# Sixteen subtractions of a two-layer hybrid block move from GpSimd to VectorE, with new instruction orders in five of its seven regions

## The chip, the cores and the metric

The kernel runs on one core of a Trainium2 chip. The metric is the device time of one execution in microseconds (us). TensorE is called PE, VectorE DVE, ScalarE ACT and GpSimd POOL in the views of the profile; SP is the sync engine, which issues most DMAs.

## The reference, cut to what matters

Two layers work on a latent sequence of 512 tokens and a context of 256, both 1024 wide, all in float32. Layer 0 mixes with a gated long convolution and a grouped-query attention; layer 1 with an mLSTM (a recurrence with a matrix state per head, here by chunks, forwards and backwards). Only the latent tokens of layer 1 are returned.

```python
for layer in range(2):
    need_ctx = layer < 1
    h_lat = rms_norm(x_lat, g_pre[layer]) * (1 + sc_l) + sh_l      # sc, sh, ga: silu(c) @ w_mod + b_mod
    h_ctx = rms_norm(x_ctx, g_pre[layer]) * (1 + sc_c) + sh_c
    if layer == 0:
        y_lat, y_ctx = even_mixer(h_lat, h_ctx, ...)               # convolution | attention, then @ e_w_out
    else:
        y_lat, _ = odd_mixer(h_lat, h_ctx, ...)
    x_lat = x_lat + ga_l * rms_norm(y_lat, g_post[layer])
    if need_ctx:
        x_ctx = x_ctx + ga_c * rms_norm(y_ctx, g_post[layer])
return x_lat

# the end of odd_mixer: 8 heads of 256 make the 2048 columns that o_w_out turns into 1024
h = (h_f + h_b) * sigmoid(o)
h = rms_norm(h per head, head_norm)
y = (h * silu(z)) @ w_out
```

## The kernel before, in words

*Number format.* Each float32 matmul is three matmuls on rounded parts: a tensor is split into a high part (`wh`, `hTh`, `yfh`; a cast on ACT) and a low part (`wl`, `hTl`, `yfl`; DVE subtracts the high part from the source), and `mm3` issues high x high, low x high and high x low into one PSUM tile. Weights come by DMA on SP into `wr` (three buffers, half a slot's columns each), ACT casts them to `wh`, DVE makes `wl`; there are two slots of `wh` and `wl`, each filled in two halves of 128x1024. A slot can be refilled when PE's last matmul on it has ended.

*Regions and orders.* The whole program is written down as calls first (`record`), cut into seven regions: `start`, `hy` (the convolution of layer 0), `att` (its attention), `out0` (its output product, the norms after it, and the norm and transposes of layer 1), `l1a` (the dense part, with the first products of layer 1), `l1b` (its scan), `out1` (its output product and the end). `play` then issues each region's calls in the order of a table, `ORDERS[region]`, and every engine keeps that order. So the tables fix which instruction follows which on each engine, and an engine stands when the next one in its row is not ready. A second table, `SLOTS`, says which of a pool's buffers each tile takes. All instructions carry the line L998 of `play`, so the views are read by the names of tiles. The digits behind a name in an order (`pm_8141`) tell one tile from another.

*Layer boundary (`out0`).* For each of six token tiles the norm gives `xt`, `sst`, `rs` and `xn` (two halves); eight transposes on PE turn `xn` into two PSUM tiles `pm` (four each); ACT and DVE each scale two of the four blocks into `hf`, and a split makes `hTh` and `hTl`, on which all of layer 1's products work. The first of these products are the 288 columns for gates and values (`wh1_1348`, `wl1_1349`, loaded as `wr_8192`, `wr_8193`, `wr_8194`).

*Output of layer 1.* It is computed with seven products instead of eight (p1, q7, q6, q3, q5, p2, q4) of blocks of the activations and of sums of weight blocks. The activations of the sums are the "forms". At the end of `l1b`, `raws` (`vh`, `vl`, `cvo`) hold the finished heads; they are split, and a difference of two halves of their columns is taken in place. In `out1`, `forms(h)` loads a pair of heads as `yraa` and `yrab`, and takes three differences: two in place on `yraa`, one into `yf`. The results are split into `yfh`/`yfl`, `ybh`/`ybl` and parts of `hTh`/`hTl`. These differences are the subtractions of the change; their instructions are 2 of 128x768, 2 of 128x256 and 12 of 128x512. In the last head groups of `l1b`, `hst` and `hrs` (on POOL) give the head norm's factor, `hh<-hh,hrs,zs` applies it, and PE transposes `hh`.

Of the kernel before, what the change touches and what calls it, by code (L numbers as in the profile page):

```python
# [151 lines left out]
class Ctx:  # L152
# [679 lines left out]
    ],  # L832
    "yraw@9": [
        0, 0, 0, 1, 1, 0, 1, 0,
    ],
    "ess@9": [
        0, 0, 0, 0, 0, 0,
# [2056 lines left out]
```

## Time and the profile before

| what | value |
|---|---|
| median of 3 runs | 1501.41 us (1500.29 to 1501.62) |
| profiled execution | 1502.13 us, its span 1500.4 us |
| mean granted clock of TensorE | 0.990 of full |
| PE, DVE, ACT, POOL busy | 1454.9, 1073.5, 779.8, 121.1 us |
| the 16 subtractions on POOL | 26.6 us |

The span goes from the first to the last instruction; 1.7 us of the execution lie around it. "Busy" is the time in which an engine had an instruction at work; durations overlap a little where an engine starts an instruction before the one ahead of it has ended. The granted clock is what the chip gave TensorE, 1.00 being full speed.

### The profile page before, as it was taken

The page shows a single profiled execution, that of the slowest core. Times are in us where ns is not written, and L with a number is a line of the kernel's source. Part 1 is how long each engine was busy: PE and PEld are TensorE (multiplying, and loading weights), DVE is VectorE, ACT ScalarE, POOL GpSimd, SP SyncE. Part 2 cuts the span into 40 slices and gives each one's busy share as a digit, 9 for nine tenths or more (in the row PEclk, how much of TensorE's full clock was granted, in tenths as well). Part 3 has the DMA queues.
Part 4 walks back from the last instruction along what each step waited for, and adds up shares of the span by engine and source line. Part 5 has one row for each costly group of instructions (what it writes and reads, how often), then busy time and mean ns, then how long its engine had stood idle before and what let it go on. Part 6 is the DMA issues. An engine that isn't in the chain of part 4 may idle for free. (4 is left out here: it accounts for less than half of the span.)

```text
span 1500.4 us, 25608 instructions
## 1 busy us (share of the span) xinstructions
PE 1454.9 (97%) x10122; PEld 1328.6 (89%) x10122; DVE 1073.5 (72%) x1955; ACT 779.8 (52%) x1587; POOL 121.1 (8%) x157
## 2 busy tenths in 40 slices
PE   7999999999999999999999889999999999999987
PEld 5889999889998999899997779999999999998765
DVE  6687777887866666768334789566777777877787
ACT  6634343434435444446332557654766666765553
POOL 1100000001000000010000100000102010011130
PEclk9999999999999999999999999999999999999999
DMA  9755565557231121242552334675866454574665
GB/s 378 214 136 146 148 163 128 146 139 187 70 99 48 49 96 54 81 138 92 187 208 67 116 119 155 225 248 198 238 183 135 112 167 122 169 196 155 240 204 202
DMA packets 63688, 230.95 MB, mean 154 GB/s; under 512 B 7707, under 2 KB 9243, under 8 KB 60784
## 3 DMA queue, kind: packets, MB, share of 16 engines
q1 hardware_dynamic: 55000, 198.63, 38.7%
q0 software_dynamic: 7696, 29.50, 10.8%
q8 instruction: 80, 1.31, 0.4%
q10 hardware_dynamic: 872, 1.18, 0.3%
q14 instruction: 40, 0.33, 0.1%
HBM read 207.23 MB, written 68.19 MB: 184 GB/s over the span
## 5 line engine op out<-in xcount | busy, mean ns | idle before, releaser
L998 PE MATMUL pj<-wl,hTh 128*128 128x256 f32 (+2 forms) x1104 | 316.5, 292 | 1.9 <-DVE wl L998 1.9
L998 PE MATMUL pj<-wh,hTh 128*128 128x256 f32 (+2 forms) x1104 | 315.6, 293 | 0.9 <-ACT qjunk L998 0.5
L998 PE MATMUL pj<-wh,hTl 128*128 128x256 f32 (+2 forms) x1104 | 314.7, 292 | 0.0
L998 PE MATMUL pj<-hTh,wh 128*128 128x512 f32 (+1 forms) x832 | 286.6, 346 | 0.2 <-DVE vl L998 0.2
L998 PE MATMUL pj<-hTl,wh 128*128 128x512 f32 (+1 forms) x832 | 285.6, 344 | 0.6 <-DVE hTl L998 0.6
L998 PE MATMUL pj<-hTh,wl 128*128 128x512 f32 (+1 forms) x832 | 285.4, 345 | 0.0
L998 DVE TENSOR_TENSOR wl<-wr,wh 128x1024 fp32r<-128x1024 f32 (+1 forms) x154 | 188.7, 1231 | 50.7 <-ACT wh L998 50.5
L998 PEld LDWEIGHTS pj<-wh,hTh 128*128 128x128 f32 x1104 | 207.0, 189 | 7.9 <-issue 2.1
L998 PEld LDWEIGHTS pj<-wl,hTh 128*128 128x128 f32 x1104 | 208.1, 190 | 6.6 <-DVE wl L998 2.6
L998 PEld LDWEIGHTS pj<-wh,hTl 128*128 128x128 f32 x1104 | 206.7, 189 | 3.9 <-issue 0.5
L998 ACT CAST wh<-wr 128x1024 fp32r<-128x1024 f32 (+1 forms) x154 | 159.0, 1044 | 71.8 <-PE pj L998 39.0
L998 PEld LDWEIGHTS pj<-hTh,wh 128*128 128x128 f32 x832 | 156.6, 189 | 18.7 <-DVE vl L998 0.8
L998 PEld LDWEIGHTS pj<-hTl,wh 128*128 128x128 f32 x832 | 156.7, 188 | 17.8 <-DVE hTl L998 0.9
L998 PEld LDWEIGHTS pj<-hTh,wl 128*128 128x128 f32 x832 | 156.3, 188 | 17.5 <-DVE wl L998 0.2
L998 ACT CAST PTh<-pj 128x384 fp32r<-128x384 f32 (+1 forms) x80 | 35.6, 459 | 49.3 <-PE pj L998 45.5
L998 DVE TENSOR_TENSOR PTl<-pj,PTh 128x384 fp32r<-128x384 f32 (+1 forms) x80 | 41.3, 525 | 22.5 <-ACT PTh L998 22.2
L998 DVE TENSOR_TENSOR wl<-ch,wh 128x1024 fp32r<-128x1024 f32 x28 | 34.0, 1219 | 26.2 <-ACT wh L998 26.2
L998 POOL DMA_DIRECT2D o_sums<-in_o_w_in x28 | 22.8, 814 | 334.5 <-DMA o_sums<-in_o_w_in 167.4
L998 DVE TENSOR_REDUCE mx<-s 128x1 f32<-128x768 f32 (+1 forms) x48 | 37.0, 774 | 14.7 <-PE s L998 14.6
L998 ACT ACTIVATE qjunk<-pj 128x128 f32<-128x128 f32 x60 | 16.7, 278 | 55.3 <-PE pj L998 23.4
L998 PE MATMUL s<-dfa,qTh 128*128 128x256 f32 (+1 forms) x160 | 45.0, 343 | 0.0
L998 PE MATMUL pm<-Rh,dfa 128*128 128x256 f32 (+1 forms) x192 | 45.0, 305 | 0.0
(397 smaller groups left out, 3313.6 us busy)
## 6 DMA issues: line engine op xcount, KB each, us to landing
wr<-in_e_w_in SPq DMA_DIRECT2D x52, 512.0 KB, 5.1
wr<-in_o_w_in SPq DMA_DIRECT2D x50, 512.0 KB, 5.6
o_sums<-in_o_w_in POOLq DMA_DIRECT2D x28, 512.0 KB, 6.6
ch<-o_sums SPq DMA_DIRECT2D x21, 512.0 KB, 5.7
wh<-in_w_mod SPq DMA_DIRECT2D x10, 1024.0 KB, 5.9
wl<-in_w_mod SPq DMA_DIRECT2D x9, 1024.0 KB, 8.1
wr<-in_e_w_out SPq DMA_DIRECT2D x16, 512.0 KB, 4.4
w_sums<-in_o_w_out POOLq DMA_DIRECT2D x16, 512.0 KB, 8.0
```

The lines of the kernel that those rows point to most:

```text
L998: x = fn(*a, **k)
```

## The change

The sixteen subtractions are issued on DVE instead of POOL. `ORDERS` of five regions (`att`, `out0`, `l1a`, `l1b`, `out1`) are other tables with the same calls, and `SLOTS` has other buffers for some pools (`wr`, `pj`, `pm`, `xt`, `xn`, `yraw`, `C` and others). `start` and `hy` are as they were. The number of instructions of each kind is the same but for the engine of the sixteen.

```diff
     for raw in raws:
         n = raw.shape[1]
         split(*[x[:, k:k + n, NL:NT] for x in hT_], raw[:, :, :256])
-        G.tensor_tensor(raw[:, :, 256:], raw[:, :, 256:], raw[:, :, :256], ALU.subtract)
+        V.tensor_tensor(raw[:, :, 256:], raw[:, :, 256:], raw[:, :, :256], ALU.subtract)
         k += n
...
-        G.tensor_tensor(ra[:, :, hi], ra[:, :, hi], rb[:, :, hi], ALU.subtract)
-        G.tensor_tensor(ra[:, :, lo], ra[:, :, lo], ra[:, :, hi], ALU.subtract)
+        V.tensor_tensor(ra[:, :, hi], ra[:, :, hi], rb[:, :, hi], ALU.subtract)
+        V.tensor_tensor(ra[:, :, lo], ra[:, :, lo], ra[:, :, hi], ALU.subtract)
         split(*[x[:, kk] for x in f6], ra[:, :, lo])
 
         def second():
             x = T(op, "yf3", (P, 2, 256), bufs=4)
-            G.tensor_tensor(x, rb[:, :, lo], ra[:, :, lo], ALU.subtract)
+            V.tensor_tensor(x, rb[:, :, lo], ra[:, :, lo], ALU.subtract)
```

Of the tables, `out1` has 426 entries of which 25 stand at their old place, moved by 10 places on average; `l1b` has 3871 of which 46 stand, moved by 38; `out0` 1028, 53 and 31; `att` 3139, 118 and 26; `l1a` 1701, 199 and 11. What that does is shown at three places.

DVE at the end of `l1b`, from the split of the head group that is normed last but one; `hst_11964` leads to `hrs_11965`, which the four `hh` need, and `wl_2364` is a weight half. Before:

```order
L998 TENSOR_SCALAR hst_11964<-hss_11959 128x4
L998 TENSOR_TENSOR vl_11835<-pj_11943,vh_11834 128x256
L998 TENSOR_TENSOR hTl<-vl_12057,hTh 128x3x256
L998 SCALAR_TENSOR_TENSOR hh_11945<-hh_11945,hrs_11965,zs_11839 128x256 x3
L998 SCALAR_TENSOR_TENSOR E_11966<-pm_11958,E_11966 128x512
L998 SCALAR_TENSOR_TENSOR hh_11945<-hh_11945,hrs_11965,zs_11839 128x256
L998 TENSOR_TENSOR El_11968<-E_11966,Eh_11967 128x512
L998 TENSOR_TENSOR vl_11835<-pj_11944,vh_11834 128x256
```

After:

```order
L998 TENSOR_TENSOR vl_11835<-pj_11943,vh_11834 128x256
L998 TENSOR_TENSOR vl_11835<-pj_11944,vh_11834 128x256
L998 SCALAR_TENSOR_TENSOR E_11966<-pm_11958,E_11966 128x512
L998 TENSOR_TENSOR wl_2364_11953<-wr_11954,wh_2363_11952 128x1024
L998 SCALAR_TENSOR_TENSOR hh_11945<-hh_11945,hrs_11965,zs_11839 128x256 x2
L998 TENSOR_TENSOR vl_12057<-vl_12057 128x3x256
L998 SCALAR_TENSOR_TENSOR hh_11945<-hh_11945,hrs_11965,zs_11839 128x256
L998 TENSOR_TENSOR El_11968<-E_11966,Eh_11967 128x512
L998 TENSOR_TENSOR wl_2364_11953<-wr_11955,wh_2363_11952 128x1024
L998 SCALAR_TENSOR_TENSOR C_11981<-C_11977,apb_9239,pj_11980 128x258
L998 SCALAR_TENSOR_TENSOR hh_11945<-hh_11945,hrs_11965,zs_11839 128x256
```

The subtraction of `vl_12057` stands between the `hh` on DVE; on POOL it stood ahead of two more subtractions. The split `hTl<-vl_12057`, which stood ahead of the `hh`, is further back, and a weight half stands ahead of them instead.

DVE at the start of `out1`: `wl_2496` is the second weight slot of q7, `wl_2519` that of q6, which follows it on PE; `gg` is the factor of the last norm. Before:

```order
L998 TENSOR_TENSOR wl_2496_12085<-wr_12086,wh_2495_12084 128x1024
L998 TENSOR_TENSOR wl_2496_12085<-wr_12087,wh_2495_12084 128x1024
L998 TENSOR_TENSOR gg_1586_11172<-pm_12054,gg_1586_11172 128x512
L998 TENSOR_TENSOR ybl_16007<-yrab_16011,ybh_16006 128x512
L998 TENSOR_TENSOR hTl<-yrab_16011,hTh 128x2x256
L998 TENSOR_TENSOR yfl_16005<-yraa_16010,yfh_16004 128x512
L998 TENSOR_TENSOR hTl<-yraa_16010,hTh 128x2x256
L998 TENSOR_TENSOR hTl<-yrab_16013,hTh 128x2x256
L998 TENSOR_TENSOR ybl_16007<-yrab_16013,ybh_16006 128x512
L998 TENSOR_TENSOR wl_2519_16017<-wr_16018,wh_2518_16016 128x1024
```

After, where two more subtractions (`yraa_16012` and `yf_2537`) stand behind these rows and ahead of `wl_2519`:

```order
L998 TENSOR_TENSOR wl_2496_12085<-wr_12087,wh_2495_12084 128x1024
L998 TENSOR_TENSOR gg_1586_11172<-pm_12054,gg_1586_11172 128x512
L998 TENSOR_TENSOR wl_2496_12085<-wr_12086,wh_2495_12084 128x1024
L998 TENSOR_TENSOR ybl_16007<-yrab_16011,ybh_16006 128x512
L998 TENSOR_TENSOR yraa_16010<-yraa_16010,yrab_16011 128x2x256
L998 TENSOR_TENSOR yraa_16010<-yraa_16010 128x2x256
L998 TENSOR_TENSOR yf_2536_16034<-yrab_16011,yraa_16010 128x512
L998 TENSOR_TENSOR hTl<-yrab_16011,hTh 128x2x256
L998 TENSOR_TENSOR yfl_16005<-yraa_16010,yfh_16004 128x512
L998 TENSOR_TENSOR hTl<-yraa_16010,hTh 128x2x256
L998 TENSOR_TENSOR hTl<-yrab_16013,hTh 128x2x256
L998 TENSOR_TENSOR yraa_16012<-yraa_16012,yrab_16013 128x2x256
```

Six operations stood between the two weights' splits; now eleven do (with the two), six of them subtractions that POOL made. The halves of `wl_2496` have changed places, with `gg` between them; PE uses the half from `wr_12086` first in both. PE from p1's last matmul to q7's first one with `wl_2496`, before:

```order
L998 MATMUL pj_12079<-wh_2485_12074,hTl 128x512
L998 MATMUL pj_12089<-wh_2491_12080,hTh 128x512
L998 MATMUL pj_12089<-wl_2492_12081,hTh 128x512
L998 MATMUL pj_12089<-wh_2491_12080,hTl 128x512
...
L998 MATMUL pj_12089<-wh_2491_12080,hTl 128x512
L998 MATMUL pj_12089<-wh_2495_12084,hTh 128x512
L998 MATMUL pj_12089<-wl_2496_12085,hTh 128x512
```

After:

```order
L998 MATMUL pj_12078<-wh_2485_12074,hTl 128x512
L998 MATMUL pm_12054<-mrow_12053,c_sel 128x512
L998 MATMUL pj_12088<-wh_2491_12080,hTh 128x512
L998 MATMUL pj_12088<-wl_2492_12081,hTh 128x512
L998 MATMUL pj_12088<-wh_2491_12080,hTl 128x512
L998 MATMUL pj_12088<-wh_2491_12080,hTh 128x512
L998 MATMUL pj_12088<-wl_2492_12081,hTh 128x512
L998 MATMUL pj_12088<-wh_2491_12080,hTl 128x512
L998 MATMUL pj_12088<-wh_2495_12084,hTh 128x512
L998 MATMUL pj_12088<-wl_2496_12085,hTh 128x512
```

The first row is p1's last matmul, the last that reads the slot of p1's second weights, `wh_2485`, which `wh_2495` takes. Thirteen rows stood between it and the first matmul with `wl_2496`; now eight do.

PE at the layer boundary: `pm_8141`, `pm_8188` and `pm_8189` are PSUM tiles of transposes, `pj_8139` and `pj_8154` belong to layer 0's output product, `pj_8195` to `pj_8197` to the 288 columns of layer 1. Before, first at `pm_8141` and then at the last two tiles:

```order
L998 MATMUL pj_8139<-wh_1254_8096,yol_8028 128x512
L998 MATMUL pm_8141<-c_ident,xn_8119 128x128 x3
L998 MATMUL pj_8154<-wh_1242_8084,yoh_8027 128x512
L998 MATMUL pm_8141<-c_ident,xn_8119 128x128
L998 MATMUL pj_8154<-wl_1243_8085,yoh_8027 128x512
...
L998 MATMUL pj_8195<-wh_1348_8190,hTl 128x288
L998 MATMUL pm_8188<-c_ident,xn_8179 128x128 x4
L998 MATMUL pm_8189<-c_ident,xn_8180 128x128 x4
L998 MATMUL pj_8195<-wh_1348_8190,hTh 128x288
```

After, at the same two places:

```order
L998 MATMUL pj_8139<-wh_1242_8084,yoh_8027 128x512
L998 MATMUL pm_8141<-c_ident,xn_8119 128x128 x4
L998 MATMUL pj_8139<-wl_1243_8085,yoh_8027 128x512
...
L998 MATMUL pj_8195<-wh_1348_8190,hTl 128x288
L998 MATMUL pm_8189<-c_ident,xn_8180 128x128
L998 MATMUL pj_8195<-wh_1348_8190,hTh 128x288
L998 MATMUL pj_8195<-wl_1349_8191,hTh 128x288
L998 MATMUL pm_8189<-c_ident,xn_8180 128x128 x2
L998 MATMUL pj_8195<-wh_1348_8190,hTl 128x288
L998 MATMUL pj_8196<-wh_1348_8190,hTh 128x288
L998 MATMUL pj_8196<-wl_1349_8191,hTh 128x288
L998 MATMUL pj_8196<-wh_1348_8190,hTl 128x288
L998 MATMUL pm_8188<-c_ident,xn_8179 128x128 x3
L998 MATMUL pj_8197<-wh_1348_8190,hTl 128x288
L998 MATMUL pm_8188<-c_ident,xn_8179 128x128
```

The four transposes of `pm_8141` follow each other, and those of the last two tiles are taken apart, with matmuls of the 288 columns between them. On DVE there, the split of the half `wr_8194` stood ahead of the last tile's two `xt` (with a product `yacc` by `gg`); it stands behind them now.

More of the change, by code (lines that the diff above doesn't have):

```diff
@@ L743 @@
     "pj@2": [
-        1, 0, 1, 0, 3, 2, 1, 3, 0, 2, 3, 1, 0, 2, 3, 1, 0, 2, 2, 1, 0, 3, 1, 2, 0, 0, 2, 0, 1, 3, 2, 0, 1, 3, 1, 0, 2, 3, 1, 0, 3, 2, 0, 2, 3, 1, 0,
-        2, 3, 1, 2, 0, 3, 1, 2, 0, 1, 3, 2, 0, 1, 3, 3, 0, 1, 2, 3, 0, 1, 1, 2, 3,
+        0, 1, 0, 1, 2, 3, 0, 2, 1, 3, 2, 0, 1, 3, 2, 0, 1, 3, 3, 0, 1, 2, 0, 3, 1, 1, 3, 1, 0, 2, 3, 1, 0, 2, 0, 1, 3, 2, 0, 1, 2, 3, 1, 3, 2, 0, 1,
+        3, 2, 0, 3, 1, 2, 0, 3, 1, 0, 2, 3, 1, 0, 2, 2, 1, 0, 3, 2, 1, 0, 0, 3, 2,
     ],
@@ L773 @@
     "rt@6": [
-        0, 1, 1, 1, 1, 1, 0, 0, 1, 0, 1, 0, 1, 0, 1, 0, 0, 1, 0, 1, 0, 1,
+        1, 0, 0, 1, 0, 1, 0, 0, 1, 1, 0, 1, 1, 0, 1, 0, 1, 1, 0, 1, 0, 1,
     ],
@@ L801 @@
     "s2@8": [
-        1, 0, 0, 1, 0, 1, 1, 0, 1, 0, 0, 1, 1, 1, 0, 1, 0, 1, 1, 0, 1, 0, 0, 1, 1, 0, 1, 0, 1, 1, 0, 0, 1, 0, 1, 1, 0, 1, 0, 1, 0, 1, 1, 0, 1, 0, 1,
+        1, 0, 1, 0, 0, 1, 1, 0, 0, 1, 0, 1, 1, 1, 0, 1, 0, 1, 1, 0, 1, 0, 1, 1, 0, 1, 0, 1, 1, 0, 0, 1, 0, 0, 1, 1, 0, 0, 1, 0, 1, 0, 0, 1, 1, 0, 1,
         0,
@@ L805 @@
     "mx@6": [
-        2, 3, 1, 0, 3, 2, 1, 0, 2, 3, 1, 0, 2, 3, 1, 2, 0, 3, 1, 2, 0, 3, 1, 2, 3, 0, 1, 2, 3, 0, 1, 3, 2, 0, 1, 3, 2, 0, 1, 3, 2, 0, 1, 3, 2, 1, 0,
-        3,
+        1, 2, 0, 3, 2, 1, 3, 0, 2, 1, 0, 3, 2, 1, 0, 2, 3, 1, 0, 2, 3, 1, 0, 2, 3, 1, 0, 2, 1, 3, 0, 2, 3, 0, 1, 3, 2, 1, 0, 2, 3, 1, 2, 0, 3, 1, 0,
+        2,
     ],
     "sm@6": [
-        1, 2, 0, 3, 2, 1, 3, 0, 2, 1, 0, 3, 2, 1, 0, 3, 2, 1, 0, 3, 1, 2, 0, 3, 1, 2, 0, 3, 1, 2, 0, 3, 1, 2, 0, 3, 1, 2, 0, 3, 1, 2, 0, 3, 1, 2, 0,
+        0, 3, 1, 2, 3, 0, 2, 1, 3, 0, 1, 2, 0, 3, 1, 2, 0, 3, 1, 2, 0, 3, 1, 2, 0, 3, 1, 2, 3, 0, 1, 2, 0, 1, 3, 0, 2, 1, 3, 2, 0, 1, 2, 3, 1, 0, 2,
         3,
@@ L816 @@
     "xt@9": [
-        0, 1, 0, 1, 0, 1, 0,
+        1, 0, 1, 0, 1, 0, 1,
     ],
     "pj@10": [
[5 rows of a table removed]
[5 rows of a table added]
     ],
     "pm@11": [
[5 rows of a table removed]
[5 rows of a table added]
     ],
     "yraw@9": [
-        0, 0, 0, 1, 1, 0, 1, 0,
+        1, 1, 0, 0, 0, 1, 1, 1,
     ],
@@ L848 @@
     "xn@9": [
-        0, 1, 0, 2, 2, 1, 0, 1, 1, 2, 0, 2,
+        1, 0, 1, 2, 2, 0, 1, 2, 0, 1, 0, 2,
     ],
@@ L857 @@
     "cvo@12": [
-        0, 2, 1, 0, 2, 1, 0, 2, 1, 0, 2, 1, 0, 2, 1, 0, 2, 1,
+        0, 1, 2, 0, 1, 2, 0, 1, 2, 0, 1, 2, 0, 1, 2, 0, 1, 2,
     ],
     "ch@13": [
-        0, 1, 0, 1, 0, 1, 0, 1, 0, 1, 0, 1, 0, 1, 0, 1, 0, 1, 0, 1, 0, 1, 0, 1, 0, 1, 0, 1,
+        1, 0, 1, 0, 1, 0, 1, 0, 1, 0, 1, 0, 1, 0, 1, 0, 1, 0, 1, 0, 1, 0, 1, 0, 1, 0, 1, 0,
     ],
     "decay@14": [
-        0, 1, 0, 1, 0, 1, 1, 0, 1, 0, 1, 0, 1, 0, 0, 1,
+        0, 1, 0, 1, 1, 0, 0, 1, 0, 1, 0, 1, 0, 1, 1, 0,
     ],
     "C@14": [
-        1, 0, 1, 0, 1, 0, 1, 0, 1, 0, 1, 0, 1, 0, 1, 0, 1, 0, 1, 0, 1, 0, 1, 0, 1, 0, 1, 0, 1, 0, 0, 1, 0, 1, 0, 1, 0, 1, 0, 1, 0, 1, 0, 1, 0, 1, 0,
+        1, 0, 1, 0, 1, 0, 1, 0, 1, 0, 0, 1, 0, 1, 0, 1, 0, 1, 0, 1, 0, 1, 0, 1, 0, 1, 0, 1, 0, 1, 0, 1, 0, 1, 0, 1, 0, 1, 0, 1, 0, 1, 0, 1, 0, 1, 0,
         1, 0, 1, 0, 1, 0, 1, 0, 1, 0, 1, 0, 1, 0, 1, 0, 1, 0, 1, 0, 1, 0, 1, 0, 1, 0, 1, 0, 1, 0, 1, 0, 1,
@@ L870 @@
     "Ch@14": [
-        1, 0, 1, 0, 0, 1, 0, 0, 1, 0, 0, 1, 1, 0, 1, 0, 0, 1, 0, 0, 1, 0, 1, 0, 0, 1, 0, 1, 0, 1, 1, 0, 1, 0, 1, 0, 1, 0, 1, 0, 1, 0, 1, 0, 1, 0, 1,
-        0, 1, 0, 0, 1, 0, 1, 0, 1, 0, 1, 0, 1, 0, 1, 0, 0,
+        1, 0, 1, 1, 0, 1, 0, 1, 0, 1, 0, 1, 0, 1, 0, 1, 1, 0, 1, 0, 0, 1, 0, 1, 0, 1, 0, 1, 0, 1, 0, 1, 1, 0, 1, 0, 1, 0, 1, 0, 1, 0, 1, 1, 0, 1, 0,
+        1, 0, 1, 1, 0, 1, 0, 1, 0, 1, 0, 1, 0, 1, 0, 1, 0,
     ],
     "Cl@14": [
-        0, 1, 0, 1, 1, 0, 1, 0, 1, 0, 0, 1, 0, 1, 0, 1, 0, 1, 0, 1, 0, 1, 0, 1, 1, 0, 1, 0, 1, 0, 0, 1, 0, 1, 0, 1, 0, 1, 0, 1, 0, 1, 0, 1, 0, 1, 0,
-        1, 0, 1, 1, 0, 1, 0, 1, 0, 1, 0, 1, 1, 0, 1, 0, 0,
+        0, 1, 0, 0, 1, 0, 0, 1, 0, 1, 0, 1, 0, 1, 0, 1, 1, 0, 1, 0, 1, 0, 1, 0, 0, 1, 0, 1, 0, 1, 0, 1, 1, 0, 1, 0, 1, 0, 1, 0, 1, 0, 1, 1, 0, 1, 0,
+        1, 0, 1, 1, 0, 1, 0, 1, 0, 1, 0, 1, 0, 1, 0, 0, 1,
     ],
```

850 rows, old and new, of tables (ORDERS, SLOTS) are left out of this document.

## The prediction

> **What bounds the kernel now.** I read the page's busy times first, then the waits of TensorE, then a table of stretches, then the timeline at each large wait.
>
> ```profile
> span 1500.4 us, 25608 instructions
> PE 1454.9 (97%) x10122; PEld 1328.6 (89%) x10122; DVE 1073.5 (72%) x1955; ACT 779.8 (52%) x1587; POOL 121.1 (8%) x157
> ...
> PE pj L998 <- DVE wl L998: 6.9, 4, 4.7
> PE pm L998 <- DVE hf L998: 3.4, 1, 3.4
> PE pm L998 <- ACT hf L998: 3.3, 2, 2.8
> PE pm L998 <- DVE hh L998: 3.3, 2, 2.3
> PE pm L998 <- DVE xn L998: 2.6, 1, 2.6
> ```
>
> PE is busy 97% of the span, and both kernels issue the same matmuls. So the change can win only the 1500.4 - 1454.9 = 45.5 us in which PE stands, and what slow clocks cost beside that. The waits are few and long: columns are total, times, longest. The table of stretches (start:end, length, busy time of each engine with its instructions, granted clock) says where they are:
>
> ```profile
> 0.00:50.00 50.00, 39.95 (x300) 30.20 (x301) 36.26 (x71) 33.03 (x52) 7.62 (x21) 1.00 0.92 350
> ...
> 750.00:800.00 50.00, 50.00 (x356) 44.67 (x356) 16.86 (x18) 15.56 (x26) 0.00 (x0) 1.00 0.47 166
> 800.00:850.00 50.00, 46.64 (x203) 37.23 (x202) 32.52 (x63) 20.19 (x42) 4.75 (x7) 0.97 0.27 97
> 850.00:900.00 50.00, 42.09 (x250) 37.22 (x249) 41.32 (x76) 29.54 (x57) 3.92 (x8) 0.93 0.36 120
> ...
> 1350.00:1400.00 50.00, 46.81 (x371) 44.74 (x371) 38.13 (x76) 28.52 (x72) 6.04 (x4) 0.93 0.43 153
> 1400.00:1450.00 50.00, 43.16 (x192) 31.23 (x191) 38.65 (x41) 25.67 (x40) 21.50 (x13) 0.93 0.69 241
> 1450.00:1500.00 50.00, 41.61 (x178) 32.85 (x176) 40.28 (x59) 22.06 (x35) 3.26 (x4) 0.95 0.59 208
> ```
>
> A full stretch has 50.00. Beside the program's first loads (10.05 us idle) and its tail (8.39), which the change leaves as they are, three places stand out: the layer boundary (800 to 900: 3.36 + 7.91), the end of layer 1's attention (1350 to 1400: 3.19) and the start of output 1 (1400 to 1450: 6.84). Each also shows a clock under 1.00. For all the rest of the span 45.5 - 39.7 = 5.8 us are left. The same view for four short stretches finds where it is halved:
>
> ```profile
> 846.40:849.80 3.40, 2.97 (x8) 2.40 (x9) 2.31 (x7) 1.60 (x3) 0.89 (x1) 0.50 0.00 0
> 873.70:880.50 6.80, 4.02 (x18) 3.75 (x18) 3.97 (x9) 3.27 (x7) 0.18 (x3) 0.50 0.79 275
> 1365.20:1372.10 6.90, 6.00 (x29) 5.89 (x28) 5.10 (x9) 4.05 (x11) 0.00 (x0) 0.51 0.22 76
> 1430.10:1436.90 6.80, 4.10 (x10) 3.27 (x11) 6.80 (x8) 0.91 (x2) 3.41 (x2) 0.50 0.58 171
> ```
>
> At half clock, half of PE's busy time is lost: 1.5, 2.0, 3.0 and 2.0 us. Each begins during or just behind one of these waits (start, busy, what, and in brackets the idle time before it and its releaser; the two matmuls at 1427 show the step at full clock):
>
> ```profile
> 846.83 0.47 PE L998 MATMUL pm<-c_ident,xn 128*128 128x128 f32 x1 [3.36 <-DVE hf L998]
> 864.34 0.40 PE L998 MATMUL pj<-wl,hTh 128*128 128x288 f32 x1 [1.38 <-DVE wl L998]
> 873.15 0.87 PE L998 MATMUL pm<-c_ident,xn 128*128 128x128 f32 x5 [2.60 <-DVE xn L998]
> 876.80 0.90 PE L998 MATMUL pm<-c_ident,xn 128*128 128x128 f32 x3 [2.78 <-ACT hf L998]
> 1364.90 0.44 PE L998 MATMUL pm<-c_ident,hh 128*128 128x128 f32 x2 [2.29 <-DVE hh L998]
> 1366.24 0.55 PE L998 MATMUL pm<-vh,Eh 128*128 128x258 f32 x1 [0.90 <-ACT Eh L998]
> 1426.97 0.40 PE L998 MATMUL pj<-wh,hTh 128*128 128x512 f32 x1
> 1427.21 0.39 PE L998 MATMUL pj<-wl,hTh 128*128 128x512 f32 x1
> 1432.80 0.80 PE L998 MATMUL pj<-wl,yfh 128*128 128x512 f32 x1 [4.73 <-DVE wl L998]
> ```
>
> Waits of 2.29 us (with 0.90 us just behind it) and more brought half clock; the 1.38 us wait did not.
>
> **The change part by part.** *The subtractions.* GpSimd loses 16 instructions, VectorE gains them. GpSimd's groups (count | busy, mean ns):
>
> ```profile
> L998 POOL TENSOR_TENSOR yf<-yrab,yraa 128x512 f32<-128x512 f32 x4 | 7.6, 1912 | 0.2
> L998 POOL TENSOR_TENSOR vl<-vl 128x768 f32<-128x768 f32 x1 | 2.2, 2208 | 0.0
> ...
> 1359.97 4.88 DVE L998 SCALAR_TENSOR_TENSOR hh<-hh,hrs,zs 128x256 f32<-128x256 f32 x3
> 1365.37 0.47 DVE L998 SCALAR_TENSOR_TENSOR hh<-hh,hrs,zs 128x256 f32<-128x256 f32 x1
> 1425.33 1.79 DVE L998 TENSOR_TENSOR hTl<-yraa,hTh 128x512 fp32r<-128x512 f32 x1
> 1430.42 2.32 DVE L998 TENSOR_TENSOR wl<-wr,wh 128x1024 fp32r<-128x1024 f32 x1
> ...
> L998 DVE TENSOR_TENSOR hTl<-hf,hTh 128x512 fp32r<-128x512 f32 x12 | 7.9, 686 | 0.4 <-ACT hTh L998 0.2
> L998 DVE TENSOR_TENSOR hTl<-vl,hTh 128x768 fp32r<-128x768 f32 x2 | 1.9, 954 | 0.4 <-ACT hTh L998 0.4
> L998 DVE TENSOR_TENSOR hTl<-cvo,hTh 128x256 fp32r<-128x256 f32 x4 | 1.7, 419 | 0.1
> L998 DVE TENSOR_TENSOR wl<-wr,wh 128x1024 fp32r<-128x1024 f32 x153 | 188.3, 1236 | 50.7 <-ACT wh L998 50.5
> L998 ACT CAST wh<-wr 128x1024 fp32r<-128x1024 f32 x153 | 158.7, 1048 | 71.8 <-PE pj L998 39.0 <-DMA wr<-w_sums 10.4 <-PE pm L998 9.3
> ```
>
> A subtraction of 128x512 on VectorE takes 0.69 us alone (`hTl<-hf`), one of 768 columns 0.95, one of 256 columns 0.42. The added work is 12 x 0.69 + 2 x 0.95 + 2 x 0.42 = 11.0 us. But VectorE runs slower while GpSimd subtracts: an `hh` takes 4.88 / 3 = 1.63 us instead of 0.47, a 512-column split 1.79 instead of 0.69, a weight split 2.32 instead of 1.24. At the two places that alone is 3 x 1.16 + 6 x 1.0 + 1.1 = 10.6 us. So VectorE's total hardly moves, and its order decides.
>
> *End of layer 1's attention.* The transposes of the last-but-one head's `hh` waited 2.29 us, `Eh` 0.90, and 3.0 us went to the clock: 6.2 us. Without GpSimd beside them the four `hh` take 4 x 0.47 = 1.9 us instead of 4.88 + 0.47 with `E` between; even with the 0.95 us subtraction of `vl` and a weight split of 1.24 in the new row, that is 4.1 us against 5.9 in the rows from 1359.97 to 1365.84. PE's transposes are now also spread further back. What remains is 0 to 1.2 us. I take -5.2; the bounds are -6.2 (all) and 0 (a new wait as long).
>
> *Start of output 1.* The wait for `wl` of q6's weights is 4.73, with 2.0 of clock: 6.7 us. In the row before it, six 512-column operations at up to 1.79 us fill VectorE; now eleven stand there. At 0.69 us they take 7.6 us, against 6 x 1.7 = 10.2 (from 1425.33 to 1430.42 three of them take 5.09), 2.6 us less, and the weight split itself is 1.1 shorter: 3.7 of the 4.73 go by durations alone, 1.0 stays. There is a price ahead of it: the split of q7's second weights was in halves in the order of their use, and PE's last matmul on the slot that they take stood 14 matmuls ahead of the first that needs them. Now the last half comes first, `gg` stands between, and the distance is 9 matmuls. Behind the slot's release stand two casts and, after `gg`, a split of the half that PE needs: about 1.05 + 1.24 + 0.69 + 1.24 = 4.2 us against 9 x 0.24 = 2.1 us of PE work (0.24 is the step from the matmul at 1426.97 to the one at 1427.21). So a new wait of 2.1 us. It lets VectorE get ahead of PE before q6's weights, and takes the 1.0 with it. Out of 6.7 I take -4.5. Bounds: -6.7 (both go), and +2.0 (the wait at q6 stays as it is, since its eleven operations also wait for casts and loads, with half of the new one on top).
>
> Of waits near 2.1 us the trace has 1.38 without half clock and 2.29 with it; I count no clock. The Trainium skill ("TensorE: Matmul & The Clock Gate", Part 1: The HAM clock gate) lets the clock fall only after an idle window of about 3.4 us; by that the new wait costs 2.1 us and no more. The trace here shows the fall sooner, behind 2.29 us and 0.90 us with matmuls between them; by its rows the same wait could cost 2.1 + 1.7 us (half of one 3.4 us stretch), and output 1 would bring -2.8.
>
> *Layer boundary (order of output 0 and the dense part).* Waits here are 3.36 + 1.38 + 2.60 + 2.78, and 3.5 of clock: 13.6 us, with about 1.1 in smaller ones (11.27 less these four). Two of them are waits inside one PSUM tile: a transpose into a tile waits for the reader of the tile's earlier transposes (`hf`). In the new row the tile with 3.36 us is written by four transposes in a row, and the last two tiles have dense matmuls between their transposes, so that 3.36 + 1.5 and 2.78 have no cause left in the order. The 2.60 for `xn` also shrinks, since the second half of the gate weights' split, 1.24 us, moved behind the last tile's `xt`. That half is the price: the dense products that now fill PE want it, and it is later by two `xt` and one `yacc`, about 2.2 us, less what PE has to do until then. I take 1.5 for it, 1.4 for the old weight wait, 1.0 for one transpose that still waits inside its tile, 1.0 for `xn`, and 1.7 for one half clock stretch: 6.6 stay of 14.7, -8. I halve the trust in a row that I can't time and take -6.5. Bounds: -11, and +3 (the weight half becomes a wait of 4 us with its clock, and only the 3.36 goes).
>
> *The rest.* Attention of layer 0 and layer 1's scan are in other orders too. Of PE's idle time 5.8 us lie there, so there is little to gain; the new tables can remove such waits or add as many, and I take 0, bounds -3 and +5. Start and tail are unchanged.
>
> Sum: -5.2 - 4.5 - 6.5 + 0 = -16.2 of the profiled execution's 1502.13 (span 1500.4, 1.7 outside it). The median of the runs is 0.7 lower, 1501.41. That gives 1485.2; I take 1486.
>
> **Rivals.** *Only the contention goes* (0.25): the new orders of output 0 win nothing net, since each wait taken away is the cover of the next; -5.2 - 4.5 gives 1491.7. For it speaks that the weight half is moved behind work on VectorE's path; against it, that the in-tile waits have nothing else behind them. *VectorE takes it back* (0.08): eleven operations stand ahead of q6's split, and four of them wait for casts and loads; output 1 gives +2, the boundary -2, the attention's end -2: 1499.4, no change that can be measured (0.2%, 3 us, is about what a measurement of this kernel can tell). For it: VectorE is busy 38.65 of 50 us in that stretch already; against: 10.6 us of that is contention. *The splits come late everywhere* (0.09, slower): VectorE splits 153 weight halves in the row above, and PE now waits for `wl` only 4 times. If the new tables of the long scans (hardly an entry is at its old place) put each split just 0.15 us later than PE's need, 153 x 0.15 = 23 us are lost against 16.2 won: 1508. It decides from 16.2 / 153 = 0.11 us a split. Against it: VectorE idles 50.5 us in all ahead of these splits, waiting for the casts, and PE's 39.0 us are a wait for the slot, so they are made as early as the slot allows, in either order.
>
> **How the numbers follow.** Forecast 0.58 (own range 1480 to 1490), contention only 0.25, taken back 0.08, slower 0.09. The range of 8 in 10 goes from 1479, between the sum and all lower bounds, to 1498: with the first two cases and a part of the third. Faster by over 0.2% (below 1498.4): 0.83; within: 0.08; slower: 0.09.
>
> **What would show it.** In the new profile: no GpSimd row of 128x512; VectorE's 512-column splits at 0.69 us also in output 1; the group `hh<-hh,hrs,zs` near 0.47 us mean; no wait of PE over 2 us for `hh`, `hf` or the `wl` of q6; a wait for q7's `wl` of about 2 us, some 18 us ahead of the first `yf` matmul; clock 1.00 around 846 and 1365 (shifted). PE's busy time falls by the half clock's share, some 6 us, its idle time by some 10. The forecast is wrong if waits at the boundary come back under other names (`wl`, `xn`), or if short waits of PE appear throughout the scans.

## The result, and the profile after

The changed kernel takes 1484.59 us (median of 4 runs, 1483.69 to 1486.4), the kernel before 1500.85 us beside it: a ratio of 0.9894, with a 95% interval of 0.9877 to 0.9911. The profiled execution took 1486.4 us, its span 1484.6. The page after, its waits of TensorE (total, times, longest) and the groups of VectorE that stand for the moved work:

```profile
span 1484.6 us, 25597 instructions
PE 1448.9 (98%) x10122; PEld 1320.5 (89%) x10122; DVE 1071.1 (72%) x1971; ACT 778.8 (52%) x1587; POOL 95.2 (6%) x141
...
PE pm L998 <- DVE xn L998: 4.0, 5, 1.0
PE pj L998 <- DVE wl L998: 1.9, 2, 1.5
PE pm L998 <- DVE wa L998: 1.6, 1, 1.6
...
L998 DVE TENSOR_TENSOR yraa<-yraa 128x512 f32<-128x512 f32 x4 | 2.8, 690 | 0.1
L998 DVE SCALAR_TENSOR_TENSOR hh<-hh,hrs,zs 128x256 f32<-128x256 f32 x32 | 15.6, 520 | 4.2 <-POOL hrs L998 4.1
```

VectorE has 16 instructions more and is busy 1071.1 us instead of 1073.5: the added subtractions (0.69 us for each of the twelve of 128x512) are paid by what the others no longer lose beside GpSimd (an `hh` takes 0.52 us on average, 0.61 before). PE's idle time fell from 45.5 to 35.7 us, and its busy time by 6.0. Half clock, which the prediction counted at 8.5 us there, is in none of the three places now (columns as before).

```profile
800.00:850.00 50.00, 48.33 (x213) 37.34 (x213) 36.17 (x69) 21.92 (x46) 5.51 (x7) 1.00 0.26 87
850.00:900.00 50.00, 45.23 (x283) 40.48 (x281) 45.10 (x83) 34.40 (x61) 3.40 (x8) 1.00 0.40 140
1300.00:1350.00 50.00, 48.46 (x362) 46.01 (x361) 37.82 (x84) 33.82 (x86) 4.99 (x8) 1.00 0.75 200
1350.00:1400.00 50.00, 48.78 (x390) 42.51 (x389) 36.02 (x76) 31.27 (x73) 3.20 (x3) 1.00 0.55 170
1400.00:1450.00 50.00, 47.96 (x200) 36.64 (x199) 44.07 (x58) 26.01 (x36) 0.00 (x0) 1.00 0.79 271
```

Both traces have 10122 matmul records, so the start of the n-th record in one can be set against that in the other. The table gives what each kernel wins (-) or loses (+) against the profile of before in each stage, in us; the experiments e1 to e11 follow in the next section. The cuts are records 2100, 5700, 5860, 6600, 9450, 9600 and 10100 (340.9, 838.6, 881.5, 977.2, 1357.5, 1381.7 and 1486.1 us before); the boundary is shown in two parts, up to its last tile's transposes and the dense part behind them. The first stage, ahead of any change, varies by -1.9 to +0.8 us and is left out. Stages that a kernel leaves as they were show how much one profile can err: up to 1.1 us, and 1.9 at the boundary, where the length of the half clock varies. The second profile of the changed kernel (e10) shows the same: 1.6 us at the boundary, where one stretch of 3.4 us at half clock is in it (as in e3) and none in the first, and up to 0.9 elsewhere.

| kernel | layer 0's attention | boundary | dense part | scan | attention's end | output 1 |
|---|---|---|---|---|---|---|
| changed | -0.1 | -9.7 | +2.8 | +2.6 | -5.7 | -5.0 |
| e1 new orders, GpSimd | +0.6 | -9.7 | +2.7 | +2.4 | -3.8 | -0.3 |
| e2 old orders, VectorE | -0.1 | +1.9 | 0.0 | 0.0 | -5.0 | -0.5 |
| e3 boundary orders only | +1.1 | -8.2 | +2.6 | -0.5 | -1.1 | +0.4 |
| e4 q7's halves | -0.1 | -9.7 | +2.8 | +2.1 | -5.7 | -5.5 |
| e5 old scan table | -0.2 | -9.7 | +2.7 | -0.3 | -5.2 | +4.4 |
| e6 four rows | 0.0 | -3.8 | +0.6 | +0.3 | -0.3 | -0.5 |
| e7 old scan, matched buffers | -0.2 | -9.7 | +2.7 | +0.2 | -5.2 | -4.9 |
| e8 load's wait moved | -0.1 | +0.2 | 0.0 | -0.4 | -5.0 | -2.3 |
| e9 four rows and weight half | 0.0 | -5.0 | +2.1 | -0.3 | -0.2 | -1.0 |
| e10 changed, second profile | -0.1 | -8.1 | +2.9 | +2.4 | -5.0 | -4.1 |
| e11 as e7, second profile | -0.2 | -9.7 | +3.2 | 0.0 | -5.2 | -4.9 |

So the gain came from the three places, and 5.4 us of it were given back between them: 2.8 in the dense part and 2.6 in the scan.

### The profile page after: what moved, and what is told of

It is laid out like the page before. It is cut to its first block, busy times and chain, and to the rows that moved or that the text cites. A ratio compares the mean times of both kernels' runs of the same rounds, so it can differ in the third digit from the quotient of the medians.

```text
span 1484.6 us, 25597 instructions
## 1 busy us (share of the span) xinstructions
PE 1448.9 (98%) x10122; PEld 1320.5 (89%) x10122; DVE 1071.1 (72%) x1971; ACT 778.8 (52%) x1587; POOL 95.2 (6%) x141
## 5 line engine op out<-in xcount | busy, mean ns | idle before, releaser
L998 DVE TENSOR_TENSOR med<-big 128x512 f32<-128x512 f32 (+1 forms) x48 | 40.4, 865 | 5.0 <-ACT big L998 4.7
```

Source lines behind the costliest of these rows:

```text
L998: x = fn(*a, **k)
```

## The experiments

**Subtractions or orders?** Two kernels take the change apart. The first has all of the new tables, but

```diff
-        V.tensor_tensor(raw[:, :, 256:], raw[:, :, 256:], raw[:, :, :256], ALU.subtract)
+        G.tensor_tensor(raw[:, :, 256:], raw[:, :, 256:], raw[:, :, :256], ALU.subtract)
```

and so with the three in `forms`:

> The changed kernel's tables of orders and buffers, with the sixteen subtractions on GpSimd as before. Theory A (contention): VectorE's operations beside GpSimd's subtractions take 1.6 to 1.8 us again instead of 0.5 to 0.7, the hh and q6's wl come late, and PE waits for them with half clock behind it: 4 to 10 us are lost at the end of the attention and the start of output 1, 1489 to 1495 us in all; the layer boundary stays as in the changed kernel. Theory B (the orders do it all, the engine of the subtractions hardly matters): 1484 to 1486 us, no wait over 2 us at these places.

1493.15 us, ratio to before 0.9942 (0.9927 to 0.9956). The timeline of VectorE and GpSimd ahead of q6's weights, and PE behind them (start, busy, what, idle time and releaser):

```profile
1416.42 1.78 DVE L1030 TENSOR_TENSOR hTl<-yraa,hTh 128x512 fp32r<-128x512 f32 x1
1418.13 1.78 DVE L1030 TENSOR_TENSOR hTl<-yrab,hTh 128x512 fp32r<-128x512 f32 x1
1419.84 3.41 DVE L1030 TENSOR_TENSOR wl<-wr,wh 128x1024 fp32r<-128x1024 f32 x2
...
1417.74 1.62 POOL L1030 TENSOR_TENSOR yraa<-yraa 128x512 f32<-128x512 f32 x1
1419.44 1.59 POOL L1030 TENSOR_TENSOR yf<-yrab,yraa 128x512 f32<-128x512 f32 x1
...
1422.17 0.50 PE L1030 MATMUL pj<-wl,yfh 128*128 128x512 f32 x1 [2.32 <-DVE wl L1030]
1436.46 0.50 PE L1030 MATMUL pj<-wh,yfh 128*128 128x512 f32 x1 [1.30 <-ACT yfh L1030]
```

The contention is back: 1.78 us for what takes 0.69 alone, and all but 0.3 of the 5.0 us of output 1 are gone. At the attention's end the new order alone keeps 3.8 of 5.7 us: three `hh` take 2.23 us there, and PE's longest wait is 0.92 us, for `C` and not for `hh`. The Trainium skill ("SBUF — State Buffer", SBUF: two separate sides) says that VectorE, in an operation with two inputs in SBUF, and GpSimd lock the port they share in turn, the loser blocked for the whole instruction; the steps agree roughly: 1.71 us from one split to the next here, against 0.60 for a split (the step in the changed kernel) and 1.26 for a GpSimd subtraction (in the kernel before, at 1430.40), each alone.

The second has the old tables with the subtractions on VectorE; its edit is the four lines of the change's diff, and nothing of the tables:

> The tables of the kernel before, with the sixteen subtractions on VectorE where their calls stand in these tables. Ten operations then stand ahead of q6's wl instead of six. Theory A (contention): the waits of 2.29 us for hh and of 4.73 us for wl shrink under 1 us and their half clock goes: 8 to 11 us won, 1490 to 1493 us; the layer boundary keeps its 13 us. Theory B (the orders do it all): the ten operations keep wl late, 1498 to 1501 us. If the fresh order of the scan is what cost the changed kernel 2.7 us between the boundary and the attention's end, that loss is not seen here.

1497.94 us, ratio 0.9975 (0.9965 to 0.9985): 3.7 us by the medians, under half of what theory A gave it. Its first half came: 5.0 us at the attention's end, and q6's `wl` late by 0.35 instead of 4.73 us. The second did not, because output 1 gave it back further on:

```profile
1424.29 0.50 PE L1030 MATMUL pj<-wl,yfh 128*128 128x512 f32 x1 [0.35 <-DVE wl L1030]
1428.43 0.50 PE L1030 MATMUL pj<-wl,yfh 128*128 128x512 f32 x1 [0.84 <-DVE wl L1030]
1432.02 0.73 PE L1030 MATMUL pj<-wh,yfh 128*128 128x512 f32 x2 [0.99 <-ACT yfh L1030]
1435.16 0.80 PE L1030 MATMUL pj<-wh,yfl 128*128 128x512 f32 x1 [1.95 <-DVE yfl L1030]
...
1433.08 0.69 DVE L1030 TENSOR_TENSOR yraa<-yraa,yrab 128x512 f32<-128x512 f32 x1 [1.17 <-DMA yraa<-y_scratch]
1433.81 0.69 DVE L1030 TENSOR_TENSOR yraa<-yraa 128x512 f32<-128x512 f32 x1
1434.42 0.69 DVE L1030 TENSOR_TENSOR yfl<-yraa,yfh 128x512 fp32r<-128x512 f32 x1
```

On VectorE a subtraction whose load is late stands ahead of the split that PE needs; on GpSimd it held up only itself. Moving two rows of the table tests that:

```diff
-   yraa_16020 (2 subtractions), yfl<-yraa_16014, wl<-wr_16030
+   yfl<-yraa_16014, wl<-wr_16030, yraa_16020 (2 subtractions)
```

> The tables of the kernel before with the subtractions on VectorE, as in the run that gave back 4 us in output 1, and two rows moved: the two in-place subtractions of the fourth pair of heads, of which the first waits 1.17 us for the load of its yraa, stand behind yfl of the third pair and a half of the next weights instead of ahead of them. Theory A (a subtraction that waits for a load held the split behind it, and half clock followed): PE's 1.95 us for yfl and the half clock go, 2 to 4 us under that run: 1494 to 1496 us. Rival (the splits are late by the sheer number of operations on VectorE): the same 1497 to 1498 us.

1494.14 us, ratio 0.9960 (0.9946 to 0.9973). The wait of 1.95 us and the half clock behind it are gone, and output 1 wins 2.3 instead of 0.5 us; the rest of the difference to the run before lies at the boundary, where the two have the same rows. Waits of 0.84 and 0.99 us stay, so the old table loses by more than this one load. Neither half of the change gives output 1's 5.0 us: -0.3 and -0.5 us apart.

**The boundary.** The tables of output 0 and the dense part alone, with their buffers, in the kernel before:

```diff
-ORDERS["out0"], ORDERS["l1a"] of before
+ORDERS["out0"], ORDERS["l1a"] of the changed kernel
```

> The kernel before with only two tables of the changed one, output 0 and the dense part of layer 1, subtractions on GpSimd. Theory A: the boundary alone brings 6.5 to 7.5 us (9.5 by the last tile, 2.3 given back in the dense part for wa and cvo), and the end stays: 1493 to 1495 us. Rival: the boundary's gain depends on what the other tables leave behind (buffers, transfers) and is under 3 us: over 1498 us.

1494.80 us, ratio 0.9951 (0.9936 to 0.9966), as theory A said: 6.9 us by the medians (5.6 by the stages of its one profile, -8.2 and +2.6), and the loss in the dense part comes with it. Which rows do it? Four transposes, moved in the old table:

```diff
-   pm_8141 x3, hf<-pm_8141, pj_8154, hf<-pm_8141, pm_8141
+   pm_8141 x4, hf<-pm_8141, pj_8154, hf<-pm_8141
...
-   pm_8189, hf<-pm_8188, hf<-pm_8189, pm_8189, hf<-pm_8188, pm_8189 x2
+   pm_8189 x4, hf<-pm_8188, hf<-pm_8189, hf<-pm_8188
```

> The kernel before with four transposes moved, nothing else: the fourth of pm_8141 and three of pm_8189 stand right behind the first ones of their tile, ahead of the hf that read the tile. Theory A (a transpose waits for a reader of its own tile that stands ahead of it in the program): the waits of 3.36 us and 2.78 us go, the half clock behind them too or in part; the 2.60 us for xn stays: 4 to 8 us are won, 1493 to 1497 us. Rival (PE has nothing else to do there, so it waits for the next xn or hTl as long): under 1.5 us won, 1500 us or more.

1496.75 us, ratio 0.9967 (0.9955 to 0.9979): 5.1 us by the medians, 3.2 by the boundary and the dense part in its one profile. PE at the two places:

```profile
847.63 0.70 PE L1030 MATMUL pm<-c_ident,xn 128*128 128x128 f32 x4 [0.91 <-DVE xn L1030]
850.98 0.73 PE L1030 MATMUL pm<-c_ident,xn 128*128 128x128 f32 x4 [2.65 <-DVE sst L1030]
...
871.07 1.26 PE L1030 MATMUL pm<-c_ident,xn 128*128 128x128 f32 x8 [2.58 <-DVE xn L1030]
```

The eight last transposes run in one go, so the 2.78 us inside the tile are gone; the 3.36 us are gone too, but 0.91 and 2.65 us of waiting for the norms of other tiles come up in their place. The new tables have more than these four rows: they fill the waits for `xn` with dense matmuls. The prediction put a price on the weight half that goes behind the last `xt`. In the old order, with the four rows:

```diff
-   wl_1349<-wr_8194, xt_8177, yacc by gg, xt_8177
+   xt_8177, yacc by gg, xt_8177, wl_1349<-wr_8194
```

> The kernel before with the four transposes moved as in the run of that name, and the split of the last weight half of the 288 columns behind the last tile's two xt on VectorE instead of ahead of them. Theory A (the xn chain is VectorE's, 1.22 us shorter): the wait of 2.58 us for the last xn falls to about 1.4, and 1 to 2.5 us more are won (half clock with it): 1494 to 1496 us. Rival (PE wants that weight half by then): a wait of 1 to 2 us for wl appears ahead of it and nothing is won: 1496.5 to 1498 us.

1497.78 us, ratio 0.9978 (0.9968 to 0.9987): nothing is won over the four rows alone. Both theories' rows are in the trace:

```profile
868.52 0.40 PE L1030 MATMUL pj<-wl,hTh 128*128 128x288 f32 x1 [1.74 <-DVE wl L1030]
872.62 1.11 PE L1030 MATMUL pm<-c_ident,xn 128*128 128x128 f32 x8 [0.97 <-DVE xn L1030]
```

The wait for `xn` fell from 2.58 to 0.97 us, and a wait of 1.74 for the weight half took its place. In the changed kernel it is 0.31; PE's own row was changed there too, and that this is the reason was not tried. The dense part gives 2.1 us back here although its table is the old one: PE comes to `wa` earlier and waits 1.84 us for it, where the kernel before has no such wait.

**The new wait for q7's weights.** The changed kernel, with the halves loaded, cast and split in the order of use (VectorE's rows):

```diff
-   wl_2496<-wr_12087, gg<-pm_12054, wl_2496<-wr_12086
+   wl_2496<-wr_12086, wl_2496<-wr_12087, gg<-pm_12054
```

> The changed kernel, with the two halves of q7's second weights loaded, cast and split in the order in which PE uses them, and gg behind both splits. Theory A: the wait of 1.54 us for this wl falls to 0 to 0.3 us, and 1.2 to 1.5 us are won: 1483 us (0.1%). Rival: the wait moves to the next weights, q6's wl, which is then as late as before: no difference.

The changed kernel has the wait, and the edit takes it away, but q6's weights are then late (the row of the changed kernel first, then that of the experiment):

```profile
1410.79 0.50 PE L998 MATMUL pj<-wl,hTh 128*128 128x512 f32 x1 [1.54 <-DVE wl L998]
```

```profile
1416.21 0.50 PE L1030 MATMUL pj<-wl,yfh 128*128 128x512 f32 x1 [0.84 <-DVE wl L1030]
```

1485.56 us (1483.59 to 1487.64), no difference from the changed kernel that these runs can tell. By the stages 0.5 us more is won in output 1, less than the 0.9 by which the changed kernel's own two profiles differ there; the rival is the nearer.

**The scan.** Its new table lost 2.4 to 2.6 us wherever it was used (the changed kernel twice and e1) and 2.1 in e4; with the old one no run lost over 0.3. So the old table was put back for this region alone, with its buffers, in the changed kernel:

```diff
-ORDERS["l1b"] of the changed kernel
+ORDERS["l1b"] of before
```

> The changed kernel, but layer 1's scan (region l1b, to q7's second weights) in the table and buffers of the kernel before; subtractions on VectorE, all other regions as changed. With the old table the two runs before lost 0 to 0.5 us between the boundary and the attention's end, with the new one 2.1 to 2.6 us. Theory A (the new scan table itself costs these 2.5 us, and out1's new table needs only the subtractions on VectorE): the scan's 2.5 us come back, the attention's end wins 5.0 instead of 5.7, output 1 wins about 5: 1482 to 1484 us, 0.1% under the changed kernel, no wait of 1.5 us for q7's wl. Rival (the tables belong together, output 1's table needs the state that the new scan table leaves): output 1 wins 0 to 2 us only, 1486 to 1489 us.

1493.62 us, ratio 0.9940 (0.9926 to 0.9954): 7 us slower than the changed kernel by the ratios to before, though the scan's loss is gone (-0.3). One wait did it, with 10.2 us of half clock from 1420.0 on:

```profile
1424.38 0.76 PE L1030 MATMUL pj<-wh,yfh 128*128 128x512 f32 x1 [8.10 <-DVE yacc L1030]
```

q6's first product waits for a buffer. The tables hold two things, an order and a choice of buffers; output 1's choice follows from which of the four PSUM buffers p1 and q7 end in, and the old end of the scan leaves them in others. Exchanging the four in output 1's list is the whole edit of the next kernel:

```diff
-SLOTS["pj"] in out1: 2, 0, 3, 1, 0, 2, 1, 3, 2, 0
+SLOTS["pj"] in out1: 1, 2, 0, 3, 2, 1, 3, 0, 1, 2
```

> The changed kernel with the old table for layer 1's scan, as in the run that stood 8.22 us at q6's first matmul, but with the four PSUM buffers of output 1 exchanged so that each tile takes the buffer of the same predecessor (q6's first two those of p1, as in both whole kernels). Theory A (that wait was for a buffer: q6's tile took the one of q7, which VectorE's yacc frees last): the 8.22 us go, the scan's 2.5 to 2.9 us stay won, output 1 wins about 5: 1481 to 1483 us, 2 to 3 us under the changed kernel. Rival (output 1's new table does not fit the old end of the scan for other reasons): a wait of over 3 us stays at q6 and the time is 1486 us or more.

The 8.10 us (8.22 in the expectation) are gone; a wait of 1.11 us for q6's `wl` is what is left there:

```profile
1417.42 0.50 PE L1030 MATMUL pj<-wl,yfh 128*128 128x512 f32 x1 [1.11 <-DVE wl L1030]
```

1484.60 us, ratio 0.9889 (0.9876 to 0.9902), not the 1481 to 1483 forecast, and no different from the changed kernel's own 0.9894. The stages put it 1.8 us ahead, so the two ran once more on one chip:

> The changed kernel once more, for a comparison on the same chip with the version with the old scan table and matched buffers: 1484 to 1486 us.

> The version with the old scan table, matched buffers and all else as changed, once more beside the changed kernel. By stages of the profiled runs it is 1.8 us ahead (2.9 us up to q7, of which 1 us is lost again at q6's wl): 1482.5 to 1484 us and under the changed kernel. Rival (the stage sums of single profiled runs mislead by as much as the start of a run varies): no difference.

The changed kernel took 1487.05 us (1485.1 to 1489.34; ratio 0.9899, 0.9881 to 0.9917), the version with the old scan 1483.94 (1483.14 to 1484.11; 0.9880, 0.9863 to 0.9898). All runs of the one lie under all of the other, while the intervals of the ratios to before overlap. On this chip the version with the old scan is the faster one, by 3.1 us of the medians; the size of the step is not better known than 0 to 3 us, since the changed kernel's first profile was 3 us shorter than its second, 1.6 of them at the boundary, which the scan's table does not touch. By the stages the scan itself is shorter by 2.4 us in both pairs, and about 1 us of that goes to the wait for q6's `wl` (1.11 and 1.32 us).

## Why the prediction was right, point by point

It said 1486.0 and 1484.59 was measured; 16.2 us were summed up for the profiled execution, and 1502.13 - 1486.4 = 15.7 came. That closeness owes something to errors that cancel, which is luck: the boundary won 3.2 us more than forecast and gave 2.8 back behind it, and the scan's loss of 2.6, put at nothing, stands against 1.4 us won beyond the forecast at the three places.

- *The subtractions cost VectorE nothing net.* Right: 0.69 us each, 1071.1 against 1073.5 us busy. The rows of e1 and e2 show the contention on and off at the same place.
- *Attention's end, -5.2.* Measured -5.7; e2 shows that the subtractions' engine alone brings 5.0 there, e1 that the order alone brings 3.8. The step was right, and either cause alone was enough for most of it.
- *Output 1, -4.5, with a new wait of 2.1 us for q7.* Measured -5.0. The wait is there, 1.54 us, with no half clock behind it, and the 1.0 left at q6 went as foreseen. That both halves of the change are needed was not said: each alone brings 0.5 or less.
- *Boundary, -6.5.* Net -6.9, but put together otherwise. The waits inside a tile were the right cause (e6), yet their terms were mis-sized: -9.7 up to the last tile. Of what was to stay, the two waits for weights took 0.31 instead of 1.5 and 1.4, the wait inside a tile 0.55 instead of 1.0, and the waits for `xn` 4.0 in five instead of 1.0. The half clock's 1.7 did not come in this profile, but it did in the second (e10), whose boundary won 8.1. The other 2.8 us were given back behind it, by waits for `wa` (1.6) and `cvo` (0.7) in the dense part, where the prediction had nothing: PE arrives earlier at work that others have not yet done, as e9 shows with the old table.
- *The rest, 0.* The step that failed. The scan's new table costs 2.6 us, inside the bounds of -3 to +5 but with a wrong middle; that the splits come late everywhere, the slower rival, is not how: PE has three waits over 0.15 us there, of 0.41, 0.39 and 1.54 us, the longest for `num` near 1328 us. They are 1.5 us more than in the kernel before; where the other 1.1 us go stays open.
- *Rivals.* "Only the contention goes" fell: the boundary's tables alone bring 6.9 us (e3), where it gave them nothing, and the subtractions with old orders bring 3.7 in all, not 9.7. "VectorE takes it back" did happen, in the old tables, by the mechanism it named (a split queued behind a subtraction that waits for a load), and it is the new order of output 1 that avoids it.
- *Half clock.* The prediction read 2.29 us and more as enough. In e1, PE waits 2.32 us and the stretch around it stays at full clock:

```profile
1419.40:1422.80 3.40, 1.08 (x5) 0.56 (x5) 3.40 (x3) 2.38 (x6) 1.67 (x2) 1.00 0.44 154
1422.80:1426.20 3.40, 3.16 (x14) 2.28 (x13) 3.40 (x3) 0.95 (x2) 3.22 (x2) 1.00 0.75 239
```

So one wait's length does not decide. The Trainium skill ("TensorE: Matmul & The Clock Gate", Part 1: The HAM clock gate) asks for an idle window of about 3.4 us; this row agrees with it, while the kernel before fell to half clock around 1365 with 2.29 and 0.90 us of waiting and matmuls between. Where the two differ the traces decide, and the last section reads the rule from them: PE need not stand for a whole such window.

## What to carry to other kernels

Work moved to an idle engine is not free if that engine slows its neighbour: here sixteen subtractions on GpSimd cost VectorE as much as doing them itself. Moving them back pays in full only together with the order (3.7 us without it), for VectorE works its row in order, and a subtraction that waits for a load holds every split behind it. And an order goes with its buffers: a good table behind another predecessor cost 8 us at a single tile until the buffers were matched.

## What the runs showed of the hardware that was not expected

A wait of 2.32 us left the clock at full speed where 2.29 and 0.90 us in a row halved it. The length of a wait is not what counts; the traces of the thirteen profiles show what does, behind the first 20 us. The clock changes at marks: the stretches at half clock start whole multiples of 3.41 us apart in every trace that has more than one (8, 144, 19 and 19 of them in the kernel before; where there is one, the marks are counted from it), and each lasts one, two or three times 3.41 us, but for the last, which the program's end cuts off. Which clock comes at a mark goes by how long PE was busy since the mark before it. Of the steps of 3.41 us at full clock, all 19 with PE busy for under 1.55 us were followed by half clock, none of 5500 with over 1.65 us was, and of the four between two were. At half clock, the 10 steps with up to 2.74 us kept it, and the 21 with 2.91 us or more brought the full clock back. The ends of matmuls are modelled in a trace, so these bounds are rough.

Steps between marks (start:end, length, PE's busy time; the clock is the third number from the end) in the kernel before, ahead of 1365 and behind it, and in e1 around its 2.32 us, which a mark at 1421.14 divides:

```profile
1361.83:1365.24 3.41, 1.12 (x9) 0.78 (x7) 3.41 (x4) 0.00 (x0) 2.74 (x2) 1.00 0.00 0
1365.24:1368.65 3.41, 2.51 (x13) 2.44 (x12) 2.76 (x5) 2.51 (x6) 0.00 (x0) 0.50 0.00 0
```

```profile
1417.73:1421.14 3.41, 2.12 (x10) 1.37 (x8) 3.41 (x3) 2.39 (x5) 3.21 (x2) 1.00 0.78 265
1421.14:1424.55 3.41, 2.38 (x10) 1.80 (x10) 3.41 (x3) 2.54 (x4) 1.75 (x2) 1.00 0.40 107
```

The marks lie differently to the program's start in each run, and that alone can decide. The changed kernel waits 0.85 and 0.98 us for `xn` at the boundary in its first profile and 0.86 and 0.98 in its second (e10). In the first a mark falls between the two waits, and the clock stays full; in the second both lie in one step, half clock follows, and the boundary wins 8.1 us instead of 9.7. The same rows, first profile and then second:

```profile
863.68:867.09 3.41, 2.24 (x15) 1.81 (x15) 2.92 (x7) 1.29 (x4) 0.86 (x1) 1.00 1.02 251
867.09:870.51 3.42, 2.44 (x20) 2.23 (x19) 2.61 (x6) 2.04 (x5) 0.24 (x3) 1.00 0.93 363
```

```profile
865.54:868.96 3.42, 1.59 (x11) 1.17 (x11) 2.32 (x7) 2.59 (x6) 0.15 (x1) 1.00 0.94 301
868.96:872.37 3.41, 3.40 (x15) 3.39 (x16) 1.48 (x3) 0.51 (x3) 0.24 (x3) 0.50 1.01 399
```

So a part of what a kernel seems to win or lose between two profiles, some 1.6 us here, is where the marks fell.
